# The heads' stage of a hybrid encoder block on TensorE: one fixed stop per column tile instead of a scheduler's order, and the Fourier tiles moved behind the heads

## The chip, the cores and the metric

The program runs on one core of a Trainium2 chip. The metric is the device time of one execution in microseconds (us). The engines of the core that matter here are TensorE (PE in the profile; PEld is its weight load), VectorE (DVE), ScalarE (ACT), GpSimd (POOL) and the queue of DMA starts on SyncE (SP). Each engine works through its own instructions in order.

## The reference

One encoder block over 1024 tokens and 16 meta tokens in front of them (1040 columns), width 1024:

```python
h = concat(meta, x)
hn = rms_norm(h, norm_g)
f_in, qkv, z, ab, gate_f, gate_d = split(hn @ w_in)
# Fourier branch: 4 groups of 128 channels
y_f = real(fft2(f_in.reshape(..., 4, 128), axes=(1, 3))) @ w_fourier
# delta branch: 8 heads of 128 channels each for q, k and v
q, k, v = split(silu(depthwise_conv_centred(qkv, conv_w)))     # 5 taps
q, k = l2_normalize(q) * 128 ** -0.5, l2_normalize(k)
g, beta = decay and gate logits, from ab, per direction
o = scan(q, k, v, g, beta) + flip(scan(flip(q), flip(k), flip(v), ...))   # chunks of 64
y_d = (rms_norm(o) * silu(z)) @ w_delta
h = h + (sigmoid(gate_f) * y_f + sigmoid(gate_d) * y_d) @ w_out
h = h + hierarchical_moe(rms_norm(h))    # 64 experts, top 2 of a group
return rms_norm(h)[:, 16:]
```

Each chunk of 64 rows in a scan needs `decay * (k k^T)`, `decay * (q k^T)` and the inverse of the triangular matrix `I + A`, A being the strict lower part of the first of these times beta. `decay` is `exp(g_i - g_j)`.

## The kernel before, in words

First the kernel normalises x and splits it into a high and a low part (`xh`, `xl`), so that a product with f32 weights is three matmuls (`xh,wh`, `xl,wh`, `xh,wl`). The gates (`gates`, L232 to L340) turn the decay logits into the sums `G`, `PL` and `FL` and write `ts`, their transposes, to a table `dF` in DRAM (L339).

The heads' stage (`heads`) goes through 24 column tiles of 128 weight columns, in batches of four heads: k0 v0 k1 q0 k2 v1 k3 q1 v2 q2 v3 q3, then the same for heads 4 to 7. Of each tile:

- `load_w` loads 512 KB of weights (`wr`) and splits them into `wh` on ACT (L860) and `wl` on DVE (L861). `product` (L220) makes 72 matmuls, in three thirds of 24 over 348, 346 and 346 columns; ACT copies each third from PSUM into `pad` (L356).
- `conv` makes the five taps: one on ACT (L369), then eight on DVE (L373, two halves by four taps). `silu_all` on ACT writes `kraw`, `vraw` or `qT`.
- `k_stage` transposes k on PE (L435, L440), ACT squares and sums it (L438), and scales it into `ktok` (L446). `k_back` transposes `ktok` back (L456) and ACT copies that to `kT` (L457). `v_stage` transposes v (L468, L471). `q_stage` sums the squares of q with 8 matmuls against ones (L481).
- `decay` fills a buffer `F` (1024 values in each of 128 partitions, of a pool with two buffers): two loads of 256 KB from `dF` on SP (L489), a difference (L494) and a minimum with a mask (L495) on DVE, an exponential on ACT (L496). `chunks` multiplies 16 chunks on PE (L508), and DVE multiplies the result into `F`: for k by two instructions (L511), after which `F` goes to `dL` (L513); for q by one (L516), after which it goes to `dQK` (L517). So a buffer `F` is free again when such a write has ended.

After a batch of four heads `inverse` loads a matrix `M` from `dL` (L529, one buffer) and `eliminate` runs 62 steps of two DVE instructions (L688, L690); four copies `mt` of the result go out of the same pool. The first elimination runs while the stage goes on.

`middle` then makes the four Fourier column tiles (the same `product`, its thirds copied to `zt` and written to `dfr`, L550 to L557), the transforms, the products of the branch gates (`project_gate`, tiles of 48 matmuls of 512 columns) and the Fourier output, while DVE runs the second elimination. From some 753 us the scan follows, then the output products, and for the last quarter of the span the experts, whose weights stream in at some 419 GB/s.

In the heads' stage and the middle a scheduler arranges each engine's instructions from priorities: the program only says in what order they are issued to it (`todo`, by tile number), and the matmuls of several tiles, the transposes and the chunk products come out mixed. In the scan (`manual_schedule` for PE) the program's own order holds on PE.

Of the kernel before, what the change touches and what calls it, by code (L numbers as in the profile page):

```python
# [112 lines left out]
class Kern:  # L113
# [235 lines left out]
    def pad_tile(self):  # L349
        nc = self.nc  # L350
        pad = self.tp.tile([128, NT + 4], F32, name="pad")
        nc.gpsimd.memset(pad[:, 0:2], 0.0)
        nc.gpsimd.memset(pad[:, NT + 2:NT + 4], 0.0)

        def ev(a, b, o):
            nc.scalar.activation(pad[:, 2 + a:2 + b], o, AF.Copy)  # L356
        return pad, ev

    def raw(self, i):

        pad, ev = self.pad_tile()
        self.project(self.io["w_t"][4 + i], 128, self.ALL, ev)
        return pad
# [18 lines left out]
    def heads(self, pad0):  # L382
        tiles = []
        for b in (0, 4):
            tiles += [(b + int(n), kind) for kind, n in ("k0 v0 k1 q0 k2 v1 k3 q1 v2 q2 v3 q3").split()]
        st = {h: {} for h in range(8)}
        todo = {}

        def at(i, f, *a):
            todo.setdefault(i, []).append((f, a))  # L390

        def conv_stage(i):
            h, kind = tiles[i]
# [8 lines left out]
        for i, (h, kind) in enumerate(tiles):  # L402
            d = st[h]
            if kind == "k":
                at(i + 2, self.k_stage, h, d)
                at(i + 2, self.decay, h, d, 1)
                at(i + 3, self.k_back, h, d)
                at(i + 3, self.chunks, h, d, 1)
                if h % 4 == 3:
                    at(i + 4, self.inverse, h - 3)  # L410
            elif kind == "v":
                at(i + 2, self.v_stage, h, d)
            else:
                at(i + 1, self.decay, h, d, 0)
                at(i + 2, self.q_stage, h, d)
                at(i + 2, self.chunks, h, d, 0)
            at(i + 1, conv_stage, i)
            for f, a in todo.pop(i, []):
                f(*a)
            d["pad" + kind] = pad0 if i == 0 else self.raw(self.COL[kind] + h)  # L420
        for i in sorted(todo):
            for f, a in todo[i]:
                f(*a)

    def k_stage(self, h, d):
        nc, ident = self.nc, self.ident
        kraw = d["kraw"]
        d["ktok"] = ktok = self.hpool.tile([128, 8, 128], F32, name="ktok")
# [55 lines left out]
    def decay(self, h, d, i):  # L484
        nc = self.nc
        d["F"] = F = self.fp.tile([128, 2, 8, 64], F32, name="F")
# [11 lines left out]
    def chunks(self, h, d, i):  # L498
        nc = self.nc
        kT, F = d["kT"], d["F"]  # L500
# [43 lines left out]
    def middle(self):  # L544
        tc, nc, io = self.tc, self.nc, self.io
        with ExitStack() as ctx:
# [5 lines left out]
            for g in range(4):  # L552
                def ev(a, b, o, g=g):
# [1220 lines left out]
```

## Time and profile before

| | us |
|---|---|
| median of three runs | 1858.05 (1855.26 to 1861.65) |
| the profiled execution | 1857.15 |
| its span | 1855.3 |
| PE busy | 1730.6 (93%) |
| DVE busy | 1043.3 (56%) |
| ACT busy | 696.9 (38%) |
| POOL busy | 188.4 (10%) |

Times in the views are counted from the start of the span. A row of a timeline is one instruction, or a run of equal ones (x4), with its start, its length and its line; brackets tell how long its engine stood idle before it and what ended that. A stretch's row gives each engine's busy time in it with the number of instructions; PEclk is TensorE's granted clock as a share of full speed, and DMA the share of time that the 16 DMA engines were busy. A row of waits says which line of an engine waited for what, the sum, how often, and the longest.

### The profile page before, as it was taken

The page shows a single profiled execution, that of the slowest core. Times are in us where ns is not written, and L with a number is a line of the kernel's source. Part 1 is how long each engine was busy: PE and PEld are TensorE (multiplying, and loading weights), DVE is VectorE, ACT ScalarE, POOL GpSimd, SP SyncE. Part 2 cuts the span into 40 slices and gives each one's busy share as a digit, 9 for nine tenths or more (in the row PEclk, how much of TensorE's full clock was granted, in tenths as well). Part 3 has the DMA queues.
Part 4 walks back from the last instruction along what each step waited for, and adds up shares of the span by engine and source line. Part 5 has one row for each costly group of instructions (what it writes and reads, how often), then busy time and mean ns, then how long its engine had stood idle before and what let it go on. Part 6 is the DMA issues. An engine that isn't in the chain of part 4 may idle for free. (4 is left out here: it accounts for less than half of the span.)

```text
span 1855.3 us, 26469 instructions
## 1 busy us (share of the span) xinstructions
PE 1730.6 (93%) x10018; PEld 1241.1 (67%) x10018; DVE 1043.3 (56%) x2195; ACT 696.9 (38%) x1539; POOL 188.4 (10%) x297
## 2 busy tenths in 40 slices
PE   7978989889999999799999999999699999999996
PEld 6968888878978887566666677888544443443342
DVE  6645558777955898456556555632634344424433
ACT  5645546444432211444444443421133232323231
POOL 2000001000010001023223100000100111001000
PEclk9998999988999999899999999999899999999998
DMA  4143542334466346734434337735499999999995
GB/s 156 51 124 114 159 137 93 101 105 134 137 198 179 122 158 206 193 106 137 146 114 128 101 117 246 224 98 216 143 402 418 419 419 419 420 419 419 420 419 204
DMA packets 149613, 395.35 MB, mean 213 GB/s; under 512 B 68151, under 2 KB 70367, under 8 KB 124511
## 3 DMA queue, kind: packets, MB, share of 16 engines
q1 hardware_dynamic: 132744, 337.65, 49.3%
q0 software_dynamic: 15248, 55.21, 9.2%
q8 instruction: 81, 1.33, 0.3%
q10 hardware_dynamic: 1488, 0.73, 0.2%
q14 instruction: 52, 0.43, 0.1%
HBM read 330.38 MB, written 65.26 MB: 213 GB/s over the span
## 5 line engine op out<-in xcount | busy, mean ns | idle before, releaser
L220 PE MATMUL proj<-xh,wh 128*128 128x346 f32 (+5 forms) x1080 | 395.9, 367 | 12.1 <-ACT pad L356 6.2
L220 PE MATMUL proj<-xl,wh 128*128 128x346 f32 (+4 forms) x1080 | 395.6, 366 | 0.0
L220 PE MATMUL proj<-xh,wl 128*128 128x346 f32 (+4 forms) x1080 | 394.0, 366 | 0.0
L220 PEld LDWEIGHTS proj<-xh,wh 128*128 128x128 f32 (+1 forms) x1080 | 208.2, 193 | 33.2 <-ACT pad L356 7.0
L220 PEld LDWEIGHTS proj<-xl,wh 128*128 128x128 f32 (+1 forms) x1080 | 208.1, 193 | 18.7 <-issue 5.8
L220 PEld LDWEIGHTS proj<-xh,wl 128*128 128x128 f32 (+1 forms) x1080 | 207.3, 192 | 19.3 <-issue 6.7
L373 DVE SCALAR_TENSOR_TENSOR acc<-pad,convw,acc 128x520 f32<-128x520 f32 x192 | 136.2, 752 | 22.2 <-ACT acc L369 22.1
L860 ACT ACTIVATE wh<-wr 128x1024 fp32r<-128x1024 f32 (+2 forms) x77 | 77.2, 1004 | 132.1 <-PE proj L220 68.2
L1336 DVE SCALAR_TENSOR_TENSOR ea<-ea,gw,gu 128x256 f32<-128x256 f32 x32 | 15.4, 480 | 176.3 <-ACT ea L1335 176.3
L861 DVE TENSOR_TENSOR wl<-wr,wh 128x1024 fp32r<-128x1024 f32 (+2 forms) x77 | 88.8, 1154 | 40.9 <-ACT wh L860 40.7
L688 DVE TENSOR_TENSOR tmp<-M 128x62 f32<-128x62 f32 (+30 forms) x124 | 105.9, 854 | 7.2 <-DMA M<-dL 5.6
L690 DVE TENSOR_TENSOR M<-M,tmp 128x62 f32<-128x62 f32 (+30 forms) x124 | 105.9, 854 | 1.8
L741 DVE SCALAR_TENSOR_TENSOR R<-main,egn,svtok 128x128 f32<-128x128 f32 x128 | 44.8, 350 | 101.6 <-PE main L739 101.5
L750 ACT ACTIVATE vd<-main,vdec 128x128 f32<-128x128 f32 x128 | 46.9, 366 | 137.0 <-PE main L748 136.8
L758 DVE SCALAR_TENSOR_TENSOR S<-S,egl,dS 128x128 f32<-128x128 f32 x240 | 72.6, 342 | 39.5 <-PE dS L757 39.1
L739 PE MATMUL main<-S,skq 128*64 128x128 f32 x1024 | 86.1, 288 | 0.1
L1335 ACT ACTIVATE ea<-gu 128x256 f32<-128x256 f32 x32 | 12.3, 384 | 187.3 <-PE gu L1331 187.3
L1361 DVE TENSOR_TENSOR yl<-dn,yh 128x512 fp32r<-128x512 f32 x64 | 44.1, 689 | 60.1 <-ACT yh L1360 60.1
L739 PEld LDWEIGHTS main<-S,skq 128*64 128x64 f32 x1024 | 54.7, 137 | 31.0 <-DVE so L761 16.9
L1360 ACT ACTIVATE yh<-dn 128x512 fp32r<-128x512 f32 x64 | 38.1, 595 | 97.8 <-PE dn L1358 97.2
L1331 PE MATMUL gu<-ml,gx 128*64 128x512 f32 x288 | 68.7, 594 | 3.0 <-DMA ml<-in_w_gu_dram 3.0
L1331 PE MATMUL gu<-mh,gx 128*64 128x512 f32 x288 | 67.0, 593 | 1.5 <-DMA mh<-in_w_gu_dram 1.5
(430 smaller groups left out, 3161.7 us busy)
## 6 DMA issues: line engine op xcount, KB each, us to landing
mh<-in_w_gu_dram SPq DMA_DIRECT2D x36, 1024.0 KB
ml<-in_w_gu_dram SPq DMA_DIRECT2D x36, 1024.0 KB
wr<-in_w_t_dram SPq DMA_DIRECT2D x52, 512.0 KB
wx<-in_w_gu_dram SPq DMA_DIRECT2D x20, 1024.0 KB
mh<-in_w_dn_dram SPq DMA_DIRECT2D x20, 1024.0 KB
ml<-in_w_dn_dram SPq DMA_DIRECT2D x18, 1024.0 KB
yh<-in_w_gu_dram SPq DMA_DIRECT2D x16, 1024.0 KB
yl<-in_w_gu_dram SPq DMA_DIRECT2D x16, 1024.0 KB
```

What stands on the lines that cost most here:

```text
L220: nc.tensor.matmul(o, w[:, k, :n], x[:, k, a:b], start=(m == 0), stop=(m == 23))
L373: nc.vector.scalar_tensor_tensor(o, pad[:, a + j:a + j + NT // 2], w[:, j:j + 1], o, op0=OP.mult, op1=OP.add)
L688: nc.vector.tensor_tensor(tv, M[:, j + 1:, j:j + 1].to_broadcast([np_, m, j]), M[:, j:j + 1, :j].to_broadcast([np_, m, j]), op=OP.mult)
L690: nc.vector.tensor_tensor(M[:, j + 1:, :j], M[:, j + 1:, :j], tv, op=OP.add)
L739: nc.tensor.matmul(ps[hs[half], i], kv[:, i, 2 * (p % 4) + half], st[half], start=True, stop=True)
L741: nc.vector.scalar_tensor_tensor(R, ps[:, 0], self.egn[:, col:col + 1], d["vtok"][p // 4][:, p % 4], op0=OP.mult, op1=OP.add)
L750: nc.scalar.activation(vd, ps[:, 2], AF.Copy, scale=self.vdec[:, col:col + 1])
L758: nc.vector.scalar_tensor_tensor(st[half], st[half], self.egl[:, half, col:col + 1], dS, op0=OP.mult, op1=OP.add)
L860: self.nc.scalar.activation(hi, src, AF.Copy)
L861: self.nc.vector.tensor_tensor(lo, src, hi.bitcast(F32), op=OP.subtract)
L1331: nc.tensor.matmul(pg[self.HS[i]], d["x"][:, 4 * kk + k, c:c + 64], w[:, 4 * i + k], start=(kk == 0 and k == 0), stop=(kk == 1 and k == 3))
L1361: nc.vector.tensor_tensor(yl[:, cs], pd, yh[:, cs].bitcast(F32), op=OP.subtract)
```

## The change

The heads' stage now runs with PE's order fixed by the program. Its loop has 28 tiles: the 24 of before, then four Fourier tiles ("f"). In each pass it issues, in this order: "early" functions (`decay`, `conv_stage`, `inverse`); the first 24 matmuls of the tile's product; the weight load of the next tile; "late" functions, always in the order `k_back`, `k_stage`, `v_stage`, `q_stage`, `chunks`; the other 48 matmuls. So PE's small work of a tile stands in one stop after its first third. Counted in tiles after the tile of a k, `k_back` comes at 4 (was 3), its `chunks` at 5 (was 3), its `decay` at 4 (was 2), `inverse` at 6 (was 4); v, q and q's `decay` keep their distances. `ktok` has two buffers (was one). A Fourier tile leaves through `pad` and one DMA of 520 KB to `dfr` (was three through `zt`), and `middle` no longer makes it. Lines move: L373 is L368 now, L431 to L529 are 13 higher, L584 to L692 and L860 to L861 are 7 higher.

```diff
@@ -346,21 +346,16 @@
         self.nc.scalar.activation(d[:, :, 0], s[:, 0:8], func)
         self.nc.scalar.activation(d[:, :, 1], s[:, 15:7:-1], func)
 
-    def pad_tile(self):
+    def pad_tile(self, bare=False):
         nc = self.nc
         pad = self.tp.tile([128, NT + 4], F32, name="pad")
-        nc.gpsimd.memset(pad[:, 0:2], 0.0)
-        nc.gpsimd.memset(pad[:, NT + 2:NT + 4], 0.0)
+        if not bare:
+            nc.gpsimd.memset(pad[:, 0:2], 0.0)
+            nc.gpsimd.memset(pad[:, NT + 2:NT + 4], 0.0)
 
         def ev(a, b, o):
             nc.scalar.activation(pad[:, 2 + a:2 + b], o, AF.Copy)
         return pad, ev
-
-    def raw(self, i):
-
-        pad, ev = self.pad_tile()
-        self.project(self.io["w_t"][4 + i], 128, self.ALL, ev)
-        return pad
 
     def conv(self, i, pad):
         nc = self.nc
@@ -380,17 +375,15 @@
     COL = {"q": 0, "k": 8, "v": 16}
 
     def heads(self, pad0):
+
         tiles = []
         for b in (0, 4):
             tiles += [(b + int(n), kind) for kind, n in ("k0 v0 k1 q0 k2 v1 k3 q1 v2 q2 v3 q3").split()]
+        tiles += [(g, "f") for g in range(4)]
         st = {h: {} for h in range(8)}
-        todo = {}
-
-        def at(i, f, *a):
-            todo.setdefault(i, []).append((f, a))
-
-        def conv_stage(i):
-            h, kind = tiles[i]
+        early, late = {}, {}
+
+        def conv_stage(h, kind):
             d = st[h]
             acc = self.conv(self.COL[kind] + h, d["pad" + kind])
             if kind == "q":
@@ -400,32 +393,52 @@
                 d[kind + "raw"] = self.hpool.tile([128, NT], F32, name=kind + "raw")
                 self.silu_all(d[kind + "raw"], acc)
         for i, (h, kind) in enumerate(tiles):
+            def at(todo, n, f, *a):
+                todo.setdefault(i + n, []).append((f, a))
             d = st[h]
             if kind == "k":
-                at(i + 2, self.k_stage, h, d)
-                at(i + 2, self.decay, h, d, 1)
-                at(i + 3, self.k_back, h, d)
-                at(i + 3, self.chunks, h, d, 1)
+                at(late, 2, self.k_stage, h, d)
+                at(early, 4, self.decay, h, d, 1)
+                at(late, 4, self.k_back, h, d)
+                at(late, 5, self.chunks, h, d, 1)
                 if h % 4 == 3:
-                    at(i + 4, self.inverse, h - 3)
+                    at(early, 6, self.inverse, h - 3)
             elif kind == "v":
-                at(i + 2, self.v_stage, h, d)
+                at(late, 2, self.v_stage, h, d)
+            elif kind == "q":
+                at(early, 1, self.decay, h, d, 0)
+                at(late, 2, self.q_stage, h, d)
+                at(late, 2, self.chunks, h, d, 0)
+            if kind != "f":
+                at(early, 1, conv_stage, h, kind)
+        order = {self.k_back: 0, self.k_stage: 1, self.v_stage: 2, self.q_stage: 3, self.chunks: 4}
+        w = None
+        for i, (h, kind) in enumerate(tiles):
+            for f, a in early.pop(i, []):
+                f(*a)
+            if i == 0:
+                st[h]["pad" + kind], gen = pad0, iter(())
             else:
-                at(i + 1, self.decay, h, d, 0)
-                at(i + 2, self.q_stage, h, d)
-                at(i + 2, self.chunks, h, d, 0)
-            at(i + 1, conv_stage, i)
-            for f, a in todo.pop(i, []):
+                pad, ev = self.pad_tile(kind == "f")
+                st[h]["pad" + kind] = pad
+                gen = self.product(w, 128, self.ALL, ev)
+                for _ in range(24):
+                    next(gen)
+            if i + 1 < len(tiles):
+                h2, k2 = tiles[i + 1]
+                w = self.load_w(self.io["w_t"][h2 if k2 == "f" else 4 + self.COL[k2] + h2], 8, 128)
+            for f, a in sorted(late.pop(i, []), key=lambda x: order[x[0]]):
                 f(*a)
-            d["pad" + kind] = pad0 if i == 0 else self.raw(self.COL[kind] + h)
-        for i in sorted(todo):
-            for f, a in todo[i]:
-                f(*a)
+            for _ in gen:
+                pass
+            if kind == "f":
+                self.nc.sync.dma_start(self.dfr[h], pad[:, 2:2 + NT])
+        assert not late and not early
 
     def k_stage(self, h, d):
         nc, ident = self.nc, self.ident
         kraw = d["kraw"]
-        d["ktok"] = ktok = self.hpool.tile([128, 8, 128], F32, name="ktok")
+        d["ktok"] = ktok = self.hpool.tile([128, 8, 128], F32, name="ktok", bufs=2)
         banks = [self.pprep.tile([128, 512], F32, name="prep") for _ in range(2)]
         ss = self.sp.tile([128, 9], F32, name="ssk")
         nc.vector.memset(ss[:, 8:9], 1.0)
@@ -483,7 +496,7 @@
 
     def decay(self, h, d, i):
         nc = self.nc
-        d["F"] = F = self.fp.tile([128, 2, 8, 64], F32, name="F")
+        d["F", i] = F = self.fp.tile([128, 2, 8, 64], F32, name="F")
         for half in range(2):
             src = self.dF[i].rearrange("(n h) a c -> n h a c", h=8)[:, h, half]
             nc.sync.dma_start(F[64 * half:64 * half + 64].rearrange("p v n c -> p (v n) c"),
@@ -497,7 +510,7 @@
 
     def chunks(self, h, d, i):
         nc = self.nc
-        kT, F = d["kT"], d["F"]
+        kT, F = d["kT"], d["F", i]
         src = kT if i == 1 else d["qT"]
         kv, qv = (t.rearrange("c (s t) -> c s t", t=64) for t in (kT, src))
         pk = self.pprep.tile([128, 512], F32, name="prep")
@@ -549,12 +562,6 @@
             pf = en(tc.tile_pool(name="pfour", bufs=3, space=PSUM))
             pc = en(tc.tile_pool(name="pchan", bufs=2, space=PSUM))
             self.zp = en(tc.tile_pool(name="zpb", bufs=2, side="right"))
-            for g in range(4):
-                def ev(a, b, o, g=g):
-                    f = self.zp.tile([128, 512], F32, name="zt")
-                    nc.scalar.activation(f[:, :b - a], o, AF.Copy)
-                    nc.sync.dma_start(self.dfr[g, :, a:b], f[:, :b - a])
-                self.project(io["w_t"][g], 128, self.ALL, ev)
             for _ in self.fourier(pf, pc):
                 pass
             for _ in self.project_gate(1):
@@ -1621,7 +1628,8 @@
                 with ExitStack() as c3:
                     self.hpool = c3.enter_context(tc.tile_pool(name="head", bufs=1))
                     self.fp = c3.enter_context(tc.tile_pool(name="fp", bufs=2))
-                    self.heads(pad0)
+                    with tc.manual_schedule(engines={mybir.EngineType.PE}):
+                        self.heads(pad0)
                 self.meta(self.pprep, en2(tc.tile_pool(name="mp", bufs=1)))
             self.middle()
             self.pproj = en(tc.tile_pool(name="pproj2", bufs=2, space=PSUM))
```

PE at the gates' products (`gg`; `prep` is the PSUM pool of all small work, `proj` that of the tiles), before:

```order
L220 MATMUL proj<-xl,wh 128x348
L220 MATMUL proj<-xh,wl 128x348
L283 MATMUL prep<-gg,cst 128x64 x2
L285 MATMUL prep<-gg,cst 128x128
L287 MATMUL prep<-gg,cst 128x128 x2
L290 MATMUL prep<-gg,cst 16x8
L291 MATMUL prep<-gg,cst 16x8
L220 MATMUL proj<-xh,wh 128x348
```

and with the change:

```order
L220 MATMUL proj<-xl,wh 128x348
L220 MATMUL proj<-xh,wl 128x348
L283 MATMUL prep<-gg,cst 128x64 x2
L285 MATMUL prep<-gg,cst 128x128
L287 MATMUL prep<-gg,cst 128x128 x2
L290 MATMUL prep<-gg,cst 16x8
L291 MATMUL prep<-gg,cst 16x8
L330 MATMUL prep<-cst,G 128x128
L448 MATMUL prep<-cst,kraw 128x128 x8
L453 MATMUL prep<-cst,kraw 16x128
L220 MATMUL proj<-xh,wh 128x346
L220 MATMUL proj<-xl,wh 128x346
```

Ahead of `gg`'s group stood 152 of the tiles' matmuls and stand 101; the transpose of `G` (L330) came 28 matmuls of a tile later and now follows it directly, with the first k's transposes behind it.

DVE at a loop of the decay tables (`F<-prep,F` are the chunk products, `F<-PL,F` and `F<-F,cst` the difference and the minimum of the next tables, `acc` is the convolution), before:

```order
L511 SCALAR_TENSOR_TENSOR F<-prep,F 128x512 x2
L482 TENSOR_SCALAR epsq<-prep 128x8
L516 TENSOR_TENSOR F<-prep,F 128x1024
L373 SCALAR_TENSOR_TENSOR acc<-pad,convw,acc 128x520 x4
L98 TENSOR_SCALAR rk_x<-ssk 128x9
L373 SCALAR_TENSOR_TENSOR acc<-pad,convw,acc 128x520 x2
L431 MEMSET ssk 128x1
L373 SCALAR_TENSOR_TENSOR acc<-pad,convw,acc 128x520 x2
L106 TENSOR_TENSOR rk_t<-rk_y 128x9
L494 TENSOR_TENSOR F<-PL,F 128x1024
L107 TENSOR_TENSOR rk_t<-rk_t,rk_x 128x9
L495 TENSOR_TENSOR F<-F,cst 128x1024
```

and with the change:

```order
L524 SCALAR_TENSOR_TENSOR F<-prep,F 128x512 x2
L529 TENSOR_TENSOR F<-prep,F 128x1024
L507 TENSOR_TENSOR F<-PL,F 128x1024
L508 TENSOR_TENSOR F<-F,cst 128x1024
L868 TENSOR_TENSOR wl<-wr,wh 128x1024
L507 TENSOR_TENSOR F<-PL,F 128x1024
L368 SCALAR_TENSOR_TENSOR acc<-pad,convw,acc 128x520 x2
L508 TENSOR_TENSOR F<-F,cst 128x1024
L368 SCALAR_TENSOR_TENSOR acc<-pad,convw,acc 128x520 x5
L98 TENSOR_SCALAR rk_x<-ssk 128x9
```

Before, eight convolution instructions stood between the last chunk product and the next table's difference; now they stand behind the first one's minimum and the second one's difference.

DVE at the start of the second elimination (`tmp<-M` and `M<-M,tmp`; `wl<-wr,wh` splits the weights of a gate tile), before:

```order
L623 TENSOR_TENSOR yF<-four,Q 128x260
L624 TENSOR_TENSOR yF<-four,Q 128x259
L584 TENSOR_TENSOR EO<-fT 128x520
L585 TENSOR_TENSOR EO<-fT 128x520
L586 TENSOR_SCALAR EO<-fT 128x1
L587 MEMSET EO 128x1
L600 TENSOR_TENSOR AB<-chan,AB 128x512
L600 TENSOR_TENSOR AB<-chan,AB 9x128
L688 TENSOR_TENSOR tmp<-M 128x62
L690 TENSOR_TENSOR M<-M,tmp 128x62
```

and with the change:

```order
L697 TENSOR_TENSOR mM<-mM,mt 8x14
L668 COPY mMt<-mM 8x256
L868 TENSOR_TENSOR wl<-wr,wh 128x1024
L695 TENSOR_TENSOR tmp<-M 128x62
L697 TENSOR_TENSOR M<-M,tmp 128x62
L695 TENSOR_TENSOR tmp<-M 128x122
L697 TENSOR_TENSOR M<-M,tmp 128x61x2
L695 TENSOR_TENSOR tmp<-M 128x180
L868 TENSOR_TENSOR wl<-wr,wh 128x1024
L697 TENSOR_TENSOR M<-M,tmp 128x60x3
```

The elimination's first five instructions came after the Fourier transform's first sums (`AB`), and now stand ahead of a `wl` of the fifth gate tile.

## Rows read from the trace of the kernel before

**Rows 1.** The page's head: the span of the execution.
```profile
span 1855.3 us, 26469 instructions
```

**Rows 2.** Stretches: length, five engines (PE, PEld, DVE, ACT, POOL), PEclk, DMA, GB/s.
```profile
85.00:450.00 365.00, 311.51 (x2196) 302.00 (x2196) 236.49 (x350) 189.63 (x429) 21.78 (x48) 0.90 0.38 118
503.00:744.00 241.00, 240.00 (x1164) 194.05 (x1162) 176.35 (x259) 55.60 (x81) 15.08 (x24) 1.00 0.54 171
```

**Rows 3.** Waits, 85 to 450 us: line <- releaser: total us, times, longest.
```profile
DVE F L494 <- DMA F<-dF: 65.9, 11, 10.8
...
PE prep L456 <- ACT ktok L446: 31.2, 7, 8.2
```

**Rows 4.** Timeline, SP's queue: start, us, line, op, out<-in [idle <-releaser].
```profile
150.57 1.25 SPq L513 DMA_DIRECT2D dL<-F  x2
...
155.53 9.39 SPq L489 DMA_DIRECT2D F<-dF  x4
```

**Rows 5.** Timeline of DVE, 149 to 174 us: one loop of the decay tables.
```profile
149.26 1.28 DVE L511 SCALAR_TENSOR_TENSOR F<-prep,F 128x512 f32<-128x512 f32 x2
...
151.66 2.76 DVE L373 SCALAR_TENSOR_TENSOR acc<-pad,convw,acc 128x520 f32<-128x520 f32 x4
...
168.08 1.22 DVE L494 TENSOR_TENSOR F<-PL,F 128x1024 f32<-128x1024 f32 x1 [10.81 <-DMA F<-dF]
...
169.34 1.22 DVE L495 TENSOR_TENSOR F<-F,cst 128x1024 f32<-128x1024 f32 x1
...
172.90 1.23 DVE L494 TENSOR_TENSOR F<-PL,F 128x1024 f32<-128x1024 f32 x1 [1.68 <-DMA F<-dF]
```

**Rows 6.** Timeline of DVE: first decay products of heads 0, 3, 4 and 7.
```profile
111.13 0.68 DVE L511 SCALAR_TENSOR_TENSOR F<-prep,F 128x512 f32<-128x512 f32 x1
...
216.91 0.68 DVE L511 SCALAR_TENSOR_TENSOR F<-prep,F 128x512 f32<-128x512 f32 x1
...
315.80 0.67 DVE L511 SCALAR_TENSOR_TENSOR F<-prep,F 128x512 f32<-128x512 f32 x1
...
443.46 0.69 DVE L511 SCALAR_TENSOR_TENSOR F<-prep,F 128x512 f32<-128x512 f32 x1 [1.63 <-PE prep L508]
```

**Rows 7.** Timeline of PE: one stop between products, 215 to 220 us.
```profile
215.06 1.15 PE L508 MATMUL prep<-kT 128*64 128x64 f32 x32
216.14 1.95 PE L481 MATMUL prep<-ones,sqq 128*128 128x1 f32 x16
...
219.10 1.09 PE L468 MATMUL prep<-cst,vraw 128*128 128x128 f32 x8
```

**Rows 8.** Stretch of PE's products (L220) alone: length, PE, PEld, PEclk, DMA.
```profile
49.10:73.00 23.90, 23.90 (x150) 23.90 (x151) 1.00 0.18 53
```

**Rows 9.** Timeline of DVE: end of the gates, first two decay tables.
```profile
70.47 0.29 DVE L277 SCALAR_TENSOR_TENSOR gg<-gsp,gea 128x136 f32<-128x136 f32 x1
...
102.67 1.23 DVE L494 TENSOR_TENSOR F<-PL,F 128x1024 f32<-128x1024 f32 x1 [7.92 <-DMA F<-dF]
...
108.65 1.23 DVE L494 TENSOR_TENSOR F<-PL,F 128x1024 f32<-128x1024 f32 x1 [2.27 <-DMA F<-dF]
```

**Rows 10.** Timeline of SP's queue: the first loads of decay tables.
```profile
89.86 9.09 SPq L489 DMA_DIRECT2D F<-dF  x4
```

**Rows 11.** Timeline of PE: the first product of tile 1.
```profile
47.68 0.32 PE L220 MATMUL proj<-xh,wh 128*128 128x348 f32 x1
```

**Rows 12.** Timeline of ACT: the last Fourier result leaves PSUM.
```profile
502.76 0.44 ACT L555 ACTIVATE zt<-proj 128x346 f32<-128x346 f32 x1
```

**Rows 13.** Timeline of SP's queue: the second elimination's four loads.
```profile
565.40 9.57 SPq L529 DMA_DIRECT2D M<-dL  x4
```

**Rows 14.** Timeline of DVE: first elimination's end, second's start.
```profile
532.11 0.22 DVE L690 TENSOR_TENSOR M<-M,tmp 128x62 f32<-128x62 f32 x1
...
579.98 0.24 DVE L688 TENSOR_TENSOR tmp<-M 128x62 f32<-128x62 f32 x1
```

**Rows 15.** Timeline of PE: the gap at the end of the middle stage.
```profile
749.33 0.79 PE L220 MATMUL proj<-xh,wh 128*128 128x512 f32 x1 [5.53 <-ACT zt L1689]
```

## The prediction

> **What bounds the kernel now.** I read the page's head first, to know what one execution has to hold: a span of 1855.3 us [rows 1]. The profiled execution took 1857.15 us, 0.9 below the median of 1858.05; the sum below is made against 1857.15. Then I read the stretches. Between 85 and 450 us PE is busy for 311.5 of 365 us, at a mean granted clock of 0.90, while from 503 to 744 us it is busy for 240.0 of 241 at full clock [rows 2]. So the heads' stage has slack in it and the middle has none: whatever the stage gains or loses up to its last Fourier tile passes to the middle one to one. The question is what PE waits for in the stage.
>
> The waits answer in two steps. PE itself waits longest for `ktok`: 31.2 us in 7 waits. But DVE, which works in order and on which `ktok`'s scale rests, waits 65.9 us in 11 waits for loads of decay tables `F` [rows 3]. The timeline shows that this is a loop. The two buffers of `F` come free when the chunk products have been multiplied in (L511 at 149.26) and written out (from 150.57); the four loads of the next two tables are issued from 155.53, and the tables are there at 168.08 and 172.90 [rows 4, 5]: 18.8 and 23.6 us after L511. For 10.81 us before 168.08 DVE does nothing. All that stands behind L494 in its order is held: convolutions, and with them silu, the transposes of k and v, and PE. That loop closes once per head; I mark it by the first L511 of a head [rows 6]. Heads 0 to 3 take (216.91 - 111.13) = 105.8 us for three loops, heads 4 to 7 (443.46 - 315.80) = 127.7: 233.5 for six, 38.9 each.
>
> **The change, part by part.** *The distances* (`k_back` a tile later, k's chunk products and `decay` two later) take the wait for `ktok` off PE: those 31.2 us are paid for work which then has over a tile, 11.4 us, to be done. But this is PE's wait; DVE's, behind it, is for a buffer whose count (two) the change leaves alone. What is late next is therefore the same loop, and each term asks where it closes now.
>
> *Start, +14.* PE's first product of tile 1 stands at 47.68 [rows 11]; 150 take 23.90 us, 0.159 each [rows 8]. In the built order 101 and not 152 stand ahead of the gates' group, which PE so reaches at 47.68 + 16.1 + 0.7 (an estimate for nine small transposes) = 64.5. Its input `gg` was made at 70.47 [rows 9], and may be ready at 69.4 as one convolution pair less stands ahead. PE waits 5 us where it had none, since now nothing may pass. In return the rows between the gates' group and FL's transposes fall from 55 to 18: 37 x 0.159 = 6 us, with 1.1 from `gg` 7 us earlier for the first load of a table, issued at 89.86 [rows 10]: 83. The tables landed at 102.67 and 108.65 [rows 9], 12.8 and 18.8 after the issue: now 96 and 102. Behind them DVE has k1's convolution (estimate 3.5) and ACT an exponential and silu (3.5): 109. PE reaches the stop of tile 4 at 69.4 + 139 x 0.159 + 4 to 8 for the small work = 96 to 100 and waits until 109 for k1's transposes. Then 1.2 (eight take 1.09), 72 matmuls (11.4), the ones (1.95) and a chunk product (1.15) [rows 7, 8]: L511 of head 0 at 125 instead of 111.13. Bounds: 0, if the wait falls on work that PE had to do anyway, and 16.
>
> *Six loops, 0.* In the new order a loop reads: L511, the second table 23.6 us later, difference and minimum (1.2 each), some five to seven convolution pieces at 0.69 [rows 5], so 30 to 31; then silu and k's scaled copies on ACT (estimate 4 to 7), and PE's stop with ones and chunk products (3 to 4) [rows 7]: 37 to 42. PE arrives there after 144 matmuls and small work, at some 26. That is the 38.9 of before within what I can tell, and I take no change. From above: the shortest that the tables' way leaves is about 34 a loop (-30 in all), and the pace of PE alone, 23 + 5 = 28 a loop, would give -65. Below: a loop of 42 gives +18.
>
> Here the Trainium skill speaks for a gain. The row has the tables landing 12.5 us after the first of the four loads was issued (155.53 to 168.08) [rows 4, 5]. Its page "DMA: Bandwidth & Descriptors", section "Anatomy of one DMA — SWDGE (gpsimd) path", puts a DMA at 2.0 us and its bytes by 436 GB/s, which would be 2.6 us for 256 KB; with that the loops would run near PE's pace. The trace disagrees for these loads, so the measured 12.5 goes into the sum.
>
> *Between the batches, -5.* Head 3's L511 to head 4's took 98.9 us [rows 6]. These are six tiles, 69 us of matmuls and some 14 of small work, and in the new order only one loop's wait falls among them: an estimated 93 to 94, between 88 and 104.
>
> *End, +10.* After head 7's L511 the stage had 59.7 us left (443.46 to 502.76 + 0.44) [rows 6, 12]. Now there are 48 + 4 x 72 = 336 matmuls, 53.4 us, 4.4 of small work, and a wait at q7's stop: its convolution stands behind the last table (18.8), difference and minimum (2.4), eight pieces (5.5), then silu and the square (8, estimate), 34 to 35, where PE arrives at 24. Together 68 to 70. Bounds 0, if the convolution gets ahead of the table, and 14. The Fourier tiles themselves cost nothing: the same 72 matmuls each, ACT's copies to `pad` as those to `zt`; 12 DMAs become 4, which are needed only by the transforms behind them.
>
> *The second elimination, +9.* In the built order its first five instructions stand ahead of the `wl` of the fifth gate tile. They need `M`, whose four loads follow the first elimination's output; they were issued at 565.40 and took 9.57, and the first step ran at 579.98, 47.9 after the first elimination's end [rows 13, 14], with other DVE work ahead of it and no wait. I take 576 for the landing. PE, with the stage ending at 503 + 19 = 522, comes to that tile after four of 48 matmuls at 0.206 (240.0 by 1164 [rows 2]) and 4 of other work: 566 to 567. It waits 9; bounds 0 and 17.
>
> *End of the middle, -5.* Before the scan PE stood idle for 5.53 us [rows 15]; a PE that comes later has no cause to. Bounds -8 and 0.
>
> Sum: 14 + 0 - 5 + 10 = 19 for the stage, + 9 - 5: 23. 1857.15 + 23 = 1880. `ktok`'s second buffer, `wr` loads issued a little earlier and the eight small fills of POOL that go cost nothing: they lie beside waits of others.
>
> **The rivals.** *A, faster:* the loops close at 34 us, since k's copies and its convolution no longer wait for PE's mixed order, so that only the tables' way is left. For it: 23.6 + 2.4 + 4 of convolution and 4 of ACT makes 34, and PE is free of its 31.2 us of waits [rows 3]. Against: v's and q's work in the same loop. 6 x -5 = -30: 1850, and 1840 if the second elimination does not wait either. It decides if the loops measure under 37.
>
> *B, much faster:* the tables land as soon as PE needs them, by the page's rule named above. Against: the measured landing [rows 4, 5]. About -60: 1820.
>
> *C, the same:* the start costs 5 rather than 14 and the end nothing, as DVE gets the convolutions ahead of the tables: 5 - 5 + 9 - 5 = 4, 1861. This is also near to where it would come out if the fixed order did nothing in the stage; that it is fixed is plain from the built order.
>
> *D, slower still:* the second elimination's wait is the full 17 (+8), and more of the stops end in a wait, so that the mean granted clock of 0.90 [rows 2] falls by 0.03 on 311 us of busy time (+9): 1897.
>
> **How the numbers follow.** The forecast, 1880, has 0.49; A 0.20, B 0.05, C 0.13, D 0.13. Some 0.3% (5.6 us) is what a measurement tells from no change here: A and B are faster (0.25), C the same (0.13), the forecast and D slower (0.62). The range, 1838 to 1902, holds D, C and A with its better end, and leaves out B and the far ends of the bounds. The forecast's own range is 1866 to 1894.
>
> **What would show it.** Right: head 0's L524 (the old L511) near 125; the six loops summing to 225 to 245; DVE still waiting some 60 us or more for `F<-dF`; the last Fourier copy near 522; a PE wait of about 9 us for a `wl` behind the second elimination near 567. Wrong in its main step: loops of 34 or less, with DVE's wait for the tables under 30 us. Wrong in its start: no wait of PE at the gates' group, or L524 at 115 or before.

## The result, and the profile after

The changed kernel takes 1911.33 us (median of four runs, 1910.31 to 1912.3), the kernel before on the same chip 1859.85 (four runs, 1855.26 to 1861.7): a ratio of 1.0281, 95% interval 1.0262 to 1.0299. It is 51 us slower. The forecast was 1880 and its range ended at 1902: right in sign, too small by more than half. The profiled execution took 1911.1 us, with this span on its page:

```profile
span 1909.0 us, 26443 instructions
```

Stretches of the changed kernel (columns as in [rows 2]):

```profile
85.00:450.00 365.00, 294.06 (x2089) 288.51 (x2089) 225.75 (x331) 172.07 (x399) 20.59 (x45) 0.87 0.37 111
203.00:213.00 10.00, 9.88 (x95) 9.75 (x96) 7.28 (x11) 1.77 (x5) 0.13 (x2) 0.60 0.33 102
450.00:530.00 80.00, 60.37 (x413) 59.30 (x412) 67.16 (x76) 27.78 (x40) 0.13 (x2) 0.81 0.32 103
551.00:804.00 253.00, 246.28 (x1192) 197.52 (x1192) 167.52 (x255) 65.83 (x89) 16.60 (x29) 0.99 0.56 178
```

Between 85 and 450 us PE is busy for 294.1 us where it was busy for 311.5 [rows 2], and the stage now goes on to 551 us. From there to the scan PE is about as full as before: 246.3 of 253 us, where it was 243.7 of 250 between 503 and 753 us. The second row is a stretch right behind a wait of PE: its granted clock is 0.60 there, so PE ran at 1.2 of its 2.4 GHz for most of it.

The waits of PE and DVE between 47 and 560 us:

```profile
PE prep L494 <- ACT sqq L491: 45.2, 5, 11.9
PE prep L481 <- ACT vraw L347: 22.2, 3, 15.5
PE prep L448 <- ACT kraw L347: 14.8, 2, 11.2
...
PE prep L283 <- DVE gg L277: 4.8, 1, 4.8
...
DVE F L507 <- DMA F<-dF: 108.7, 13, 16.2
```

and DVE's in the kernel before, in the same stretch:

```profile
DVE F L494 <- DMA F<-dF: 67.2, 12, 10.8
DVE F L494 <- issue: 25.4, 4, 8.7
```

PE's waits for `ktok` [rows 3] are gone, as forecast. In their place it waits 45.2 us for the squares of q, 22.2 for silu of v and 14.8 for silu of k: 82.2 us at three kinds of fixed stops. All three stand behind a convolution, and DVE behind the tables: 108.7 us in 13 waits, where it had 67.2 in 12 before. The second row of before is idle time ahead of the same instruction for which the profile names no releaser; in the changed kernel that is 1.0 us. With it DVE's idle time ahead of the tables' arithmetic went from 92.6 to 109.7 us, a smaller rise than the named waits alone suggest.

The marks that the prediction named, on DVE's timeline (heads 0, 3, 4 and 7, as [rows 6]), then ACT's last Fourier copy, then PE at the gates' group and at k1's stop:

```profile
129.97 0.68 DVE L524 SCALAR_TENSOR_TENSOR F<-prep,F 128x512 f32<-128x512 f32 x1
...
250.45 0.69 DVE L524 SCALAR_TENSOR_TENSOR F<-prep,F 128x512 f32<-128x512 f32 x1 [0.41 <-PE prep L521]
...
345.51 0.67 DVE L524 SCALAR_TENSOR_TENSOR F<-prep,F 128x512 f32<-128x512 f32 x1
...
478.93 0.68 DVE L524 SCALAR_TENSOR_TENSOR F<-prep,F 128x512 f32<-128x512 f32 x1
```

```profile
550.99 0.44 ACT L357 ACTIVATE pad<-proj 128x346 f32<-128x346 f32 x1
```

```profile
69.35 0.90 PE L283 MATMUL prep<-gg,cst 128*128 128x64 f32 x3 [4.82 <-DVE gg L277]
...
111.07 1.33 PE L448 MATMUL prep<-cst,kraw 128*128 128x128 f32 x5 [11.15 <-ACT kraw L347]
```

| term | forecast | measured |
|---|---|---|
| start, head 0's mark against 111.13 | +14 | +18.8 |
| six loops: 120.5 + 133.4 = 253.9 against 233.5 | 0 | +20.4 |
| between heads 3 and 4: 95.1 against 98.9 | -5 | -3.8 |
| end: 478.93 to 551.43, 72.5 against 59.7 | +10 | +12.8 |
| the stage: 551.43 against 503.20 | +19 | +48.2 |
| all behind the stage: spans 1909.0 and 1855.3, less 48.2 | +4 | +5.5 |

A head's mark comes two tiles later in the program's order than before (its chunk products moved from 3 to 5 tiles), so the terms for start and end hold this shift too; the loops between marks do not.

One term holds most of the miss: the six loops. One by one they took 38.1, 34.0, 33.6 (heads 0 to 3) and 40.3, 50.6, 36.8 us (heads 4 to 7) before, and take 40.2, 38.5, 41.8 and 50.4, 36.8, 46.1 now. The first three hold 14.7 us of the 20.4. The second loop, from 170.16 to 208.64 (38.5 us where it was 34.0), on DVE, ACT and PE:

```profile
188.04 1.22 DVE L507 TENSOR_TENSOR F<-F,G 128x1024 f32<-128x1024 f32 x1 [9.77 <-DMA F<-dF]
189.18 1.43 DVE L368 SCALAR_TENSOR_TENSOR acc<-pad,convw,acc 128x520 f32<-128x520 f32 x2
190.52 1.22 DVE L508 TENSOR_TENSOR F<-F,cst 128x1024 f32<-128x1024 f32 x1
191.66 3.44 DVE L368 SCALAR_TENSOR_TENSOR acc<-pad,convw,acc 128x520 f32<-128x520 f32 x5
```

```profile
188.01 1.28 ACT L509 ACT_TABLE_LOAD   x1 [5.00 <-DMA F<-dF]
191.77 1.06 ACT L509 ACTIVATE F<-F 128x1024 f32<-128x1024 f32 x1 [2.48 <-DVE F L508]
...
195.87 0.63 ACT L346 ACTIVATE qT<-acc 128x512 f32<-128x512 f32 x1 [0.67 <-DVE ssk L444]
...
198.34 2.17 ACT L459 ACTIVATE ktok<-prep,rk_y 128x128 f32<-128x128 f32 x8 [0.38 <-DVE rk_y L109]
...
202.02 1.04 ACT L491 ACTIVATE sqq<-qT 128x1024 f32<-128x1024 f32 x1
```

```profile
203.12 3.57 PE L494 MATMUL prep<-ones,sqq 128*128 128x1 f32 x16 [9.87 <-ACT sqq L491]
```

The table, q1's, lands at 188.04, 17.9 us after the mark, when DVE has stood idle for 9.77 us. Behind it come difference and minimum, and the convolution of q, whose last pieces end near 196. ACT had been held by the same load (5.00 us, at an instruction of its exponential's line L509; `ACT_TABLE_LOAD` is not a load of a decay table), then does its exponential, silu (195.87), eight scaled copies of k (198.34) and the square (202.02). PE, which had waited 9.87 us, goes on at 203.12, 15.1 us after the landing. The eight matmuls against ones (x16 in the row) take 3.57 us there, where [rows 7] has 1.95 for the same; the granted clock of 0.60 in this stretch is what differs in the rows.

### The profile page after: what moved, and what is told of

Its sections match the earlier page's. It is cut to its first block, busy times and chain, and to the rows that moved or that the text cites. A ratio compares the mean times of both kernels' runs of the same rounds, so it can differ in the third digit from the quotient of the medians.

```text
span 1909.0 us, 26443 instructions
## 1 busy us (share of the span) xinstructions
PE 1739.2 (91%) x10018; PEld 1251.5 (66%) x10018; DVE 1048.7 (55%) x2195; ACT 694.0 (36%) x1534; POOL 188.6 (10%) x297
## 4 chain that ended last, share of the span: by engine, by line
PE 55%; DMA 28%; DVE 9%; ACT 3%; issue 3%; SPq 2%; POOL 0%; POOLq 0%; DVEq 0%; ACTq 0%
PE proj L220 20%; PE proj L874 9%; DMA F<-dF 6%; PE main L746 4%; PE gu L1338 4%; DMA ml<-in_w_gu_dram 3%; DVE acc L368 3%; PE main L767 3%; PE dS L764 3%; DMA mh<-in_w_dn_dram 2%; DMA yl<-in_w_gu_dram 2%; DMA mh<-in_w_gu_dram 2%; DMA wx<-in_w_gu_dram 2%; DMA yh<-in_w_gu_dram 2%; PE dn L1365 2%
## 5 line engine op out<-in xcount | busy, mean ns | idle before, releaser
L220 PE MATMUL proj<-xh,wh 128*128 128x346 f32 (+5 forms) x1080 | 394.6, 366 | 8.6 <-ACT pad L357 7.6
L220 PE MATMUL proj<-xl,wh 128*128 128x346 f32 (+4 forms) x1080 | 392.3, 363 | 0.0
L220 PE MATMUL proj<-xh,wl 128*128 128x346 f32 (+4 forms) x1080 | 392.1, 364 | 0.0
L220 PEld LDWEIGHTS proj<-xh,wh 128*128 128x128 f32 (+1 forms) x1080 | 207.5, 192 | 29.6 <-ACT pad L357 8.3
L220 PEld LDWEIGHTS proj<-xh,wl 128*128 128x128 f32 (+1 forms) x1080 | 206.6, 191 | 20.0 <-issue 7.0
L220 PEld LDWEIGHTS proj<-xl,wh 128*128 128x128 f32 (+1 forms) x1080 | 207.1, 192 | 17.9 <-issue 5.6
L368 DVE SCALAR_TENSOR_TENSOR acc<-pad,convw,acc 128x520 f32<-128x520 f32 x192 | 135.9, 750 | 6.8 <-ACT acc L364 6.8
L765 DVE SCALAR_TENSOR_TENSOR S<-S,egl,dS 128x128 f32<-128x128 f32 x240 | 72.5, 343 | 46.8 <-PE dS L764 46.5
L746 PEld LDWEIGHTS main<-S,skq 128*64 128x64 f32 x1024 | 54.4, 136 | 30.8 <-DVE so L768 17.5
## 6 DMA issues: line engine op xcount, KB each, us to landing
wx<-in_w_gu_dram SPq DMA_DIRECT2D x20, 1024.0 KB, 20.4
```

Source lines behind the costliest of these rows:

```text
L220: nc.tensor.matmul(o, w[:, k, :n], x[:, k, a:b], start=(m == 0), stop=(m == 23))
L368: nc.vector.scalar_tensor_tensor(o, pad[:, a + j:a + j + NT // 2], w[:, j:j + 1], o, op0=OP.mult, op1=OP.add)
L746: nc.tensor.matmul(ps[hs[half], i], kv[:, i, 2 * (p % 4) + half], st[half], start=True, stop=True)
L765: nc.vector.scalar_tensor_tensor(st[half], st[half], self.egl[:, half, col:col + 1], dS, op0=OP.mult, op1=OP.add)
```

## The experiments

Each run has its median, and the ratio to the kernel before on the same chip with its 95% interval. Times of the stage are from each run's own profiled execution, and sums of waits are from its stretch of 47 to 560 us. A theory or rival named in an expectation is the one described there, not one of the prediction's A to D.

### More buffers for the tables

```diff
-self.fp = c3.enter_context(tc.tile_pool(name="fp", bufs=2))
+self.fp = c3.enter_context(tc.tile_pool(name="fp", bufs=4))
```

> The changed kernel with four buffers F instead of two, nothing else. Theory A (the loop of the decay tables: in the fixed order PE's stops stand behind convolutions that wait in DVE's order behind loads which wait for a free buffer): with a buffer always free the loads start a tile or more earlier, DVE's wait for F<-dF falls from 108.7 us to under 30, the six loops of L524 fall from 254 us to 170 to 190, and the time to 1835 to 1855 us. Theory B (the stops cost because one fixed stop per tile leaves PE nothing else to do while DVE and ACT finish a tile, whatever the tables do): the loops stay above 230 and the time above 1890.

Measured: 1905.52 us, 1.0240 (1.0219 to 1.0261). Theory A as it stood is wrong, and so is its number for DVE's wait. The same loop in this run:

```profile
184.30 1.62 SPq L502 DMA_DIRECT2D F<-dF  x2
```

```profile
197.35 1.23 DVE L507 TENSOR_TENSOR F<-F,G 128x1024 f32<-128x1024 f32 x1 [10.97 <-DMA F<-dF]
...
DVE F L507 <- DMA F<-dF: 82.6, 12, 14.8
...
DVE F L507 <- issue: 27.5, 4, 9.7
...
262.72 1.22 DVE L529 TENSOR_TENSOR F<-prep,F 128x1024 f32<-128x1024 f32 x1
```

DVE still waits 82.6 us, and 10.97 at the same place. With the 27.5 us ahead of the same line whose releaser the profile does not name it is 110.1 us, where the changed kernel has 109.7. The loops are no shorter either: 40.0, 39.6 and 42.9 us for the first three. The loads now run two heads ahead (the table of 197.35 is first used at 262.72), but the scheduler puts each table's arithmetic right behind its load in DVE's order as well, so DVE waits for a table that it needs much later. A free buffer moves the load; it does not move the wait out of the way.

> The kernel before with four buffers F instead of two. Theory A: the same loop bounds it too, so PE's 31 us of waits for ktok and the low clock behind them mostly go: 1815 to 1835 us. Theory B says nothing of this kernel beyond that its mixed order already hides the tables: within 10 us of 1859.

Measured: 1891.32 us, 1.0164 (1.0140 to 1.0188): slower, which neither theory expected. Its six loops take 230.5 us in all, like before, but heads 3 to 4 take 118.3 us instead of 98.9. What made that stretch longer was not followed.

### The parts of the change

The scheduler's order for PE, all else as changed:

```diff
-with tc.manual_schedule(engines={mybir.EngineType.PE}):
-    self.heads(pad0)
+self.heads(pad0)
```

> The changed kernel with PE left to the scheduler again; distances, Fourier tiles and two buffers F as changed. If the fixed order is what turns the loop into lost PE time (theory A, and B): near the kernel before, 1850 to 1870 us. Rival C (the later chunk products and decay tables lengthen the loop itself): 1895 to 1915.

Measured: 1874.03 us, 1.0063 (1.0042 to 1.0084), a little over the range given. Of the 51 us, the fixed order so makes 37. The stage ends at 502.6 us, as before it (503.2): the six loops take 238.2 us instead of 253.9 with the fixed order.

```profile
PE proj L220 <- ACT pad L357: 23.9, 6, 10.3
PE prep L481 <- ACT vraw L347: 21.0, 4, 8.5
PE prep L494 <- ACT sqq L491: 10.8, 3, 7.2
```

DVE waits almost as long for the tables here (93.4 us), but PE only 31.8 us for silu and the squares, where the fixed order has 82.2. Of the 48.9 us by which the fixed order's stage ends later, 15.7 lie in the six loops and 23.8 behind head 7's mark. Of what this run is over the kernel before (17.5 us by the spans), 11.5 stand by the scan's start, at 764.5 instead of 753.0 with the stage's end unchanged, so in the middle stage; which wait makes that was not tried.

The old distances in the fixed order:

```diff
-at(early, 4, self.decay, h, d, 1)
-at(late, 4, self.k_back, h, d)
-at(late, 5, self.chunks, h, d, 1)
+at(early, 2, self.decay, h, d, 1)
+at(late, 3, self.k_back, h, d)
+at(late, 3, self.chunks, h, d, 1)
...
-at(early, 6, self.inverse, h - 3)
+at(early, 4, self.inverse, h - 3)
```

> The changed kernel with the fixed order but k's decay, k_back, chunk products and the inverse at their old distances (2, 3, 3 and 4 tiles). Theory A: the loop is no shorter and PE waits for ktok as well, which now nothing may pass: 1910 to 1940 us. Rival C: back to 1860 to 1875.

Measured: 1953.95 us, 1.0497 (1.0478 to 1.0516), beyond the expected range. PE waits for `ktok` again, and twice as long as before:

```profile
PE prep L469 <- ACT ktok L459: 63.9, 7, 14.7
```

So the longer distances are worth 43 us to a fixed order, and rival C of this expectation, in which they are the loss, is out.

The Fourier tiles back in the middle (the list of tiles without "f", the loop of L550 to L557 as before, the small work of the last head tiles issued behind the head tiles):

> The changed kernel with the four Fourier tiles made in the middle stage as before, the fixed order for the 24 head tiles alone. The prediction has these tiles at no cost: 1906 to 1917 us. Rival: in the middle the scheduler uses them to fill PE's last stops (q7's wait of 7.7 us among them): 1895 to 1905.

Measured: 1904.05 us, 1.0222 (1.0196 to 1.0248), the rival's range. The moved tiles so cost 7 us by the medians and 11 by the two ratios, where the prediction had nothing. PE's waits for the squares between 450 and 560 us, first in the changed kernel, then in this run:

```profile
PE prep L494 <- ACT sqq L491: 19.6, 2, 11.9
```

```profile
PE prep L498 <- ACT sqq L495: 13.2, 2, 11.7
```

The shorter of the two waits falls from 7.7 to 1.5 us, as the rival said. From head 7's mark to the last Fourier copy this run takes 69.7 us, the changed kernel 72.5. The rest is not located: the profiled execution, 1909.21 us, is the longest of this run's four.

### The place of the tables' arithmetic

The loads stay where they are; the arithmetic is issued a tile later and reads a column made from the convolution issued just before (`z` is 1 or -1).

```diff
+at(early, 5, self.decay_exp, h, d, 1)
...
+at(early, 2, self.decay_exp, h, d, 0)
...
+for f, a in sorted(early.pop(i, []), key=lambda x: x[0] == self.decay_exp):
...
+def decay_exp(self, h, d, i):
...
+    z = self.sp.tile([128, 1], F32, name="z")
+    nc.vector.tensor_scalar(z, self.last_acc[:, NT - 1:NT], 0.0, (1.0, -1.0)[i], op0=OP.mult, op1=OP.add)
-    nc.vector.tensor_tensor(F, *((F, c) if i == 0 else (c, F)), op=OP.subtract)
+    nc.vector.scalar_tensor_tensor(F, F, z, c, op0=OP.mult, op1=(OP.subtract, OP.add)[i])
```

> The changed kernel; the loads of a decay table stay where they are, but its difference, minimum and exponential are issued a tile later and read a column made from the convolution issued just before them, so DVE and ACT cannot have them ahead of that convolution. Two buffers as before. Theory A2 (not the number of buffers but the place of this arithmetic in DVE's and ACT's order, right behind a load of some 12 us and ahead of a convolution that a fixed stop of PE needs): DVE's wait for F<-dF falls from 108.7 us to under 30, PE's waits for sqq, vraw and kraw from 82 us to under 25, the six loops to 180 to 200 us, the time to 1800 to 1850. Theory B (one fixed stop per tile costs, whatever the tables do): over 1890 us.

Measured: 1817.20 us, 0.9776 (0.9746 to 0.9806): 94 us less than the changed kernel, with two buffers and the same fixed order.

```profile
DVE F L516 <- DMA F<-dF: 6.1, 3, 5.0
...
PE prep L497 <- ACT sqq L494: 9.0, 3, 3.6
...
PE prep L484 <- ACT vraw L347: 2.6, 2, 1.3
```

```profile
85.00:450.00 365.00, 346.17 (x2607) 341.65 (x2606) 308.43 (x443) 205.51 (x445) 18.91 (x47) 0.97 0.44 139
```

DVE's wait falls from 108.7 to 6.1 us, PE's for the squares from 45.2 to 9.0 and for v from 22.2 to 2.6; none is listed for `kraw`. The clock is 0.97 instead of 0.87. The six loops take 85.8 + 99.2 = 185.1 us. The wait for `gg` (4.8) stays, as it should. Theory B is out as the cause of the loss: the order is as fixed as before.

> The same edit with PE left to the scheduler (distances and Fourier tiles of the change). If with the tables out of the way the fixed order is worth nothing or less, as theory B has it: 1800 to 1840 and below the run with the fixed order. Theory A2: within 15 us of that run on either side, as both come near the pace of PE's work.

Measured: 1798.69 us, 0.9667 (0.9644 to 0.9689). With the tables out of the way the scheduler's order beats the fixed one by 18.5 us, slightly more than the 15 given to theory A2, and as the other reading had it: the fixed order costs something of its own. Half of its 37 us went with the tables' arithmetic behind the convolutions; the runs with the copied table below do not bear this split out.

> The kernel before, the same edit at its old distances. Theory A2: it bounds this kernel too, through ktok, 1815 to 1845 us. If the mixed order hid the tables: 1855 to 1865.

Measured: 1834.64 us, 0.9856 (0.9825 to 0.9887). The loop bounds the kernel before as well. Against the run just above, which differs in the distances, in `ktok`'s second buffer and in the Fourier tiles, this is 36 us more: once DVE is free, these parts of the change are together a gain.

### The length of the load

A copy of the table in DRAM, made once, in which a head's values are one run of 4 KB for each partition instead of 16 runs of 256 B:

```diff
+self.dG = self.dram("dG", [2, 8, 2, 16, 64])
+for i in (1, 0):
+    nc.sync.dma_start(self.dG[i], self.dF[i].rearrange("(n h) a c -> h a n c", h=8))
...
-    src = self.dF[i].rearrange("(n h) a c -> n h a c", h=8)[:, h, half]
+    src = self.dG[i][h, half].rearrange("n c -> (n c)")
...
-                      src.unsqueeze(0).to_broadcast([64, 16, 64]))
+                      src.unsqueeze(0).to_broadcast([64, 1024]))
```

> The changed kernel with the table dF copied once into an order in which a head's table is one run of 4 KB per partition instead of 16 runs of 256 B; the arithmetic on the tables stays ahead of the convolutions. Theory A2: what holds DVE is the length of the load (12 us from issue to landing); if short runs make that length, the tables land some 3 to 6 us after their issue, DVE's wait for F falls from 108.7 us to under 50, the six loops from 254 to 180 to 215, the time to 1820 to 1865 us. If the length comes from elsewhere (the queue, other transfers): 1895 to 1915.

Measured: 1844.87 us, 0.9897 (0.9865 to 0.9929). The loads between 85 and 500 us, first in the changed kernel, then in this run (the last column is the median time from issue to landing):

```profile
F<-dF SPq DMA_DIRECT2D x29, 256.0 KB, 11.7
```

```profile
F<-dG SPq DMA_DIRECT2D x30, 256.0 KB, 4.2
...
DVE F L510 <- DMA F<-dG: 35.7, 9, 8.8
...
PE prep L497 <- ACT sqq L494: 22.7, 5, 7.0
```

The same 256 KB land in 4.2 us instead of 11.7 (medians). DVE's wait falls to 35.7 us, PE's for the squares to 22.7, the six loops to 208. So it was the landing time, through DVE's order: the order was not touched here. Each load also holds SP's queue for less time (at most 2.4 us, where it was up to 5.8), which this run does not separate.

> The kernel before with the same copy. If short runs make the length: 1820 to 1845 us. If not: 1855 to 1868.

Measured: 1814.78 us, 0.9733 (0.9702 to 0.9765): the simple cure alone is worth 47 us to the kernel before.

> The distances and Fourier tiles of the change, PE left to the scheduler, with the copy of the table. If short runs make the length: 1790 to 1820 us and 10 to 40 below the run with the fixed order. If not: 1868 to 1880, as without the copy.

Measured: 1798.65 us, 0.9654 (0.9623 to 0.9685), 46 us under the run with the fixed order where 10 to 40 were given. So with short landings the fixed order costs no less than the 37 us that it costs with long ones; 18.5, 37 and 46 us are what it cost in three settings, and how much of that goes through the tables stays open.

> The fastest run so far (scheduler's order, the tables' arithmetic behind the convolution, 1798.7 us) with the copy too. Theory A2: PE there waits under 10 us in the heads' stage, so little is left: 1785 to 1800. Over 1805 if the copy's own wait at the start counts.

Measured: 1787.40 us, 0.9599 (0.9566 to 0.9633): the fastest of all, 4.0% under the kernel before. Both cures, the change's distances and Fourier tiles, and PE left to the scheduler:

```profile
85.00:450.00 365.00, 364.26 (x2738) 355.03 (x2738) 312.77 (x481) 212.25 (x467) 22.13 (x48) 1.00 0.47 148
```

PE is busy for 364.3 of 365 us at full clock, and the stage ends at 416.9 us instead of 503.2. Of these 86 us, 75 reach the end of the program.

## Why the prediction was right or wrong

**The views were read rightly in the main.** The stage holds the loss, PE's waits for `ktok` go, DVE's wait for the tables stays and PE's stops fall behind it, and what the stage loses passes on: all of this is in the profile after, and the runs on the tables' arithmetic and on the long runs show from two sides that DVE's wait for the tables is what PE's stops wait for. In one point the mechanism was wrong: I saw the loop closed by a buffer "whose count (two) the change leaves alone", and four buffers left the first three loops at 39.6 to 42.9 us. What closes it is the landing of a load whose arithmetic stands ahead of the convolutions in DVE's order.

**The step that failed is "Six loops, 0".** It measured +20.4, outside even the bound of +18 that I had put, and 253.9 us lie outside the 225 to 245 named as a sign. The comparison failed before the estimate did. My 37 to 42 us for a loop hold for the first three (40.2, 38.5, 41.8). But I held them against 38.9, a mean over two batches that differ, and took no change; the first three loops of before took 105.8 us together, 35.3 each, and against these the same estimate gives +5 to +20. They measured +14.7, and the second batch +5.7. Inside the loops:

- *ACT behind the table.* I put its part at 4 to 7 us, for silu and k's copies. In the loop shown it is held by the table too, and from landing to PE's restart 15.1 us pass, where my terms add up to 10 to 14: difference, minimum and convolution end 8 us after the landing, ACT takes the other 7. The loop still closed at 38.5 us, as this table landed 17.9 us after the mark and not 23.6: two errors offset each other, which was luck.
- *The second batch of heads.* Its first loop, marked at 345.51, takes 50.4 us. Its second table landed 34.9 us after the mark: its buffer came free only when `dQK` had been written out.

```profile
351.55 1.31 SPq L502 DMA_DIRECT2D F<-dF  x2
352.96 1.40 SPq L530 DMA_DIRECT2D dQK<-F  x1
365.51 1.29 SPq L502 DMA_DIRECT2D F<-dF  x2
```

```profile
380.41 1.23 DVE L507 TENSOR_TENSOR F<-PL,F 128x1024 f32<-128x1024 f32 x1 [9.17 <-DMA F<-dF]
...
395.95 1.28 DVE L524 SCALAR_TENSOR_TENSOR F<-prep,F 128x512 f32<-128x512 f32 x2
```

  My estimate had no such loop, but it is no part of the loss: the kernel before has one of 50.6 us (head 5's), with the same order on SP's queue. The steps of the elimination stand between the convolutions in both.

```profile
356.14 1.27 DVE L511 SCALAR_TENSOR_TENSOR F<-prep,F 128x512 f32<-128x512 f32 x2
...
406.71 0.68 DVE L511 SCALAR_TENSOR_TENSOR F<-prep,F 128x512 f32<-128x512 f32 x1
```

```profile
363.52 1.57 SPq L517 DMA_DIRECT2D dQK<-F  x1
376.46 1.29 SPq L489 DMA_DIRECT2D F<-dF  x2
```

- *"That is the 38.9 of before within what I can tell."* The 38.9 was the mixed order's at the old distances. At the new distances the mixed order takes 116.1 and 122.1 us for the two batches, the fixed one 120.5 and 133.4. So of the 14.7 us in the first batch 10.4 come without the fixed order, which adds 4.3 there and 11.3 in the second. That PE in a fixed order cannot go on to the next product while a stop waits, so that ACT and DVE get their next tile later too and PE starts again at a lower clock, is how I read the loop shown; no run separates these parts.

**The start** was right in its two waits, its total mis-sized by 4.8 us: PE waited 4.82 us at the gates' group (5 forecast) and went on at k1's stop at 111.07 (109 forecast). **Between the batches** and **the end** came within 3 us of their values. **The Fourier tiles**, put at nothing because their work stays the same, cost 7 to 11 us: in the middle stage the scheduler had them to fill PE's wait at q7's stop.

**The second elimination** did not hold PE. DVE did wait for its load, but PE, 29 us later than in my sum, was not yet at the tile that this could hold; its waits from 551 us to the scan are under 7 us in all:

```profile
587.52 0.27 DVE L695 TENSOR_TENSOR tmp<-M 128x62 f32<-128x62 f32 x1 [9.99 <-DMA M<-dL]
```

The gap of 5.53 us before the scan is gone, as forecast. That +4 behind the stage is near the +5.5 measured is luck all the same: of the two terms that make it one did not come, and in its place the middle is 2.9 us longer (551.43 to 804.1, before 503.20 to 753.0) and the scan 3.3 (804.1 to 1150.0, before 753.0 to 1095.6), neither of them traced further.

**The clock** was taken as equal. It was 0.87 against 0.90 from 85 to 450 us, and 0.81 from 450 to 530, where PE had run at full clock before.

**The rivals.** A, faster by shorter loops, was the wrong direction; its 34 us a loop came true only where the tables were cured. B's short landing came near with runs of 4 KB. C is out: the start cost 18.8 and the end 12.8 us. D, slower still, had the nearest time; its falling clock came, its long wait in the second elimination did not. The Trainium skill's page "DMA: Bandwidth & Descriptors", in the section named in the prediction, would have 2.6 us for 256 KB, an estimate from a fit for DMAs issued from GpSimd, while these loads are issued from SyncE; the trace has 11.7 for runs of 256 B and 4.2 for runs of 4 KB, so it disagrees with the first and comes nearer to the second. By that fit rival B would have been the forecast, and the measured landing was rightly put above it.

## What to carry to other kernels

A fixed order on one engine makes every stop wait for the slowest engine behind it, so first look at what stands in those engines' orders ahead of the work that the stop needs. Here it was arithmetic on a loaded table, placed as if the load were short: four buffers instead of two took 6 us off the changed kernel and added 30 to the one before, while a dependence on the work that should go first took off 94 and a load in longer runs 66. And when a wait repeats, price it loop by loop, and hold an estimate against the loops that it describes: here a mean over two unlike batches hid 14.7 us.

## What the runs showed of the hardware

- The same 256 KB from DRAM, spread to 64 partitions, land in 11.7 us (median, changed kernel) as runs of 256 B and in 4.2 us (same kernel with the copied table) as runs of 4 KB. The Trainium skill's page "DMA: Bandwidth & Descriptors", section "Why small descriptors are slow (HBM only)", gives an overhead of 27% on the DMA engine's internal bus for a descriptor of 256 B, and 32 bytes of descriptor metadata for each DMA operation besides; the trace has a factor of 2.8 for the landing of these loads, so more than that is at work, and which part was not tried apart.
- After a wait of PE of 9.87 us, the eight matmuls against ones took 3.57 us where [rows 7] has 1.95, with a granted clock of 0.60 in the 10 us from there.
